# Part of one block's load moved to GpSimd's DMA queue, with unequal shares for the DMA engines

## The chip, the cores and the metric

The kernel runs on one core of one Trainium2 chip. Five engines work beside each other: TensorE (PE, matrix products), VectorE (DVE), ScalarE (ACT), GpSimd (POOL) and SyncE (SP). Data moves between HBM and the on-chip memory SBUF through 16 DMA engines, which all queues of the core share. The metric is the device time in microseconds (us); lower is better.

## The reference

A linear layer with a low-rank update whose weights are normalised by column and rescaled, applied to 32768 rows of 256 numbers:

```
W_adapted = W + scale * (lora_A @ lora_B)          # 256x256, rank 16
W_norm    = sqrt(sum(W_adapted**2, axis=0) + 1e-8)
W_final   = W_adapted / W_norm * m
y         = x.reshape(-1, 256) @ W_final           # x: 16 x 2048 x 256, float32
```

The weights are small. x is 32 MB and y is 32 MB, both in float32, and each is moved once.

## The kernel before, in words

The 32768 rows are cut into 8 blocks of 4096 rows (4 MB). In a block each of the 128 partitions holds 32 consecutive rows of 1 KB. A chunk is 4 of these rows on all partitions, so a block has 8 chunks, and the kernel counts 64 chunks in all; two chunks are a pair. SBUF has five block buffers (`x_bufs`). A result is written over the rows that it came from, so blocks 0 to 4 have fresh buffers, and block 5 can only be loaded when block 0 has been stored.

For each pair of chunks GpSimd rounds the rows to bfloat16 (L208), TensorE transposes them (L321), VectorE copies the transposed rows from PSUM (L248), TensorE multiplies them by the final weights (L335), and ScalarE copies the result over the rows of x (L276). The final weights are computed at the start.

The order of the transfers is written out by hand. All loads go on SyncE's queue (L169 to L178), in the order of the list `loads` (L111 to L114), whose entries are a first chunk, a number of chunks and the rows of one transfer. All stores go on ScalarE's queue (`stores`, L116 to L122, whose fourth entry is the chunk after which they are issued). With `H` = 40 (the first chunk of block 5), block 4 is loaded as six chunks in one transfer of 24 rows, then, after SyncE has waited for store 0 (block 0), as two transfers of 4 rows:

```
loads += [(H - CH, 6, 6 * J), (H - 2, 2, J)]
...
if loads[n][0] == H - 2:
    wait_store(nc.sync, 0)
```

The loads of blocks 5 to 7 follow on the same queue, behind that wait and further ones. GpSimd goes through the pairs in order (L193). Before a pair it waits for the load of its chunks where a new load begins (L196), and at pair `REST` = 15 it waits for store 2 (L204), which holds back the rest of the computation while transfers go on. At the end SyncE waits for the last stores (L359). Eight and 24 waits that hold nothing up lengthen the programs of GpSimd and VectorE (L255).

Of the kernel before, what the change touches and what calls it, by code (L numbers as in the profile page):

```python
# [11 lines left out]
def kernel(  # L12
# [10 lines left out]
    nc = tc.nc  # L23
    P = 128
# [5 lines left out]
    x_flat = x.flatten_outer_dims()  # L30
    out_flat = out.flatten_outer_dims()
    N, IN = x_flat.shape
# [3 lines left out]
    J = 4  # L36
    DJ = 32
# [5 lines left out]
    XBUFS = 5  # L43
    CH = DJ // J
# [4 lines left out]
    NXB = 2  # L49

    REST = 15
    NXT = 2
    F8 = 2 * J * P

# [7 lines left out]
    def sb(name, shape, dtype):  # L62
        return ctx.enter_context(nc.sbuf_tensor(name, shape, dtype))
# [4 lines left out]
    x_bufs = [sb(f"x_sb{k}", [P, DJ, IN], FP32) for k in range(XBUFS)]  # L68
    xb_bufs = [sb(f"xb{k}", [P, 2 * J, IN], BF16) for k in range(NXB)]
    xt_bufs = [sb(f"xt{k}", [P, F8, KC], BF16) for k in range(NXT)]  # L70
    w_nat = sb("w_nat", [P, KC, OUT], FP32)
# [38 lines left out]
    H = XBUFS * CH  # L110
    loads = [(0, 2, 2 * J), (2, 2, 2 * J), (4, 4, 4 * J)]  # L111
    loads += [(b * CH, CH, CH * J) for b in range(1, XBUFS - 1)]
    loads += [(H - CH, 6, 6 * J), (H - 2, 2, J)]
    loads += [(g0, 4, 4 * J) for g0 in range(H, NCH, 4)]  # L114
    load_of = {g: n for n, (g0, cnt, _) in enumerate(loads) for g in range(g0, g0 + cnt)}
    stores = [(b * CH, CH, CH * J, 19 + b) for b in range(F - 1)]  # L116
# [7 lines left out]
    def pieces(entry):  # L124

        return 16 * (entry[1] * J // entry[2])
# [5 lines left out]
    def sem(name):  # L132
        if name not in sems:
            sems[name] = tc.alloc_semaphore(name)
        return sems[name]

    def transfer(engine, name, entry, dram, store):
        g0, cnt, rows = entry[:3]
        b, c = divmod(g0, CH)
        (u0, ucnt), = [u for u in units if u[0] <= g0 < u[0] + u[1]]  # L140
        unit = dram[u0 * J * P : (u0 + ucnt) * J * P].rearrange("(p j) k -> p j k", p=P)
        for r in range(0, cnt * J, rows):
            here = x_bufs[b % XBUFS][:, c * J + r : c * J + r + rows, :]
            there = unit[:, (g0 - u0) * J + r : (g0 - u0) * J + r + rows, :]
            src, dst = (here, there) if store else (there, here)
            engine.dma_start(out=dst, in_=src).then_inc(sem(name), 16)

    def load_x(n):
        transfer(nc.sync, f"load{n}", loads[n], x_flat, False)

    def store_y(n):
        transfer(nc.scalar, f"store{n}", stores[n], out_flat, True)

    def wait_load(engine, g):
        engine.wait_ge(sem(f"load{load_of[g]}"), pieces(loads[load_of[g]]))

    def wait_store(engine, n):
        engine.wait_ge(sem(f"store{n}"), pieces(stores[n]))
# [3 lines left out]
        out=w_nat[:], in_=W.rearrange("(p t) o -> p t o", t=KC)  # L162
    ).then_inc(sem("load_w"), 16)
    nc.scalar.dma_start(
        out=a_nat[:], in_=lora_A.rearrange("(p t) r -> p t r", t=KC)
# [2 lines left out]
    nc.scalar.dma_start(out=m_row[:], in_=m[None, :]).then_inc(sem("load_m"), 16)  # L168
    for n in range(len(loads)):  # L169

        if loads[n][0] == H - 2:
            wait_store(nc.sync, 0)
        if loads[n][0] == H + CH:
            wait_store(nc.sync, 1)
        if loads[n][0] == H + 2 * CH:
            wait_store(nc.sync, 2)
            wait_store(nc.sync, 3)
        load_x(n)  # L178
# [5 lines left out]
        out=identity[:],  # L184
        in_=zeros[:],
# [7 lines left out]
    for p in range(1, NPR):  # L193
        b, c = divmod(p, PRB)
        for g in (2 * p, 2 * p + 1):
            if g == 2 or load_of[g - 1] != load_of[g]:  # L196
                wait_load(nc.gpsimd, g)


        if p == 1:  # L200
            nc.gpsimd.wait_ge(sem("dve"), 6)
        if p == 2:
            nc.gpsimd.wait_ge(sem("dve"), 8)
        if p == REST:  # L204
            wait_store(nc.gpsimd, FIRST - 2)
        if p >= NXB:
            nc.gpsimd.wait_ge(sem("turned"), p - NXB + 1)
        nc.gpsimd.tensor_copy(  # L208
            out=xb_bufs[p % NXB][:],
            in_=x_bufs[b % XBUFS][:, 2 * c * J : 2 * (c + 1) * J, :],  # L210
        ).then_inc(sem("rounded"), 1)
# [14 lines left out]
        out=wa[:], in0=ab_ps, scalar=float(scale), in1=w_nat[:], op0=ALU.mult, op1=ALU.add  # L226
# [19 lines left out]
    for p in range(NPR):  # L246
        nc.vector.wait_ge(sem("turned"), p + 1)
        nc.vector.tensor_copy(  # L248
            out=xt_bufs[p % NXT][:].rearrange("p r t -> p (r t)").bitcast(FP32),
            in_=xt_ps[p % 2][:],  # L250
# [4 lines left out]
    for engine, idle in ((nc.gpsimd, 8), (nc.vector, 24)):  # L255
# [13 lines left out]
        out=norm[:], in_=n2_ps, func=AF.Sqrt, bias=eps_col[:]  # L269
    ).then_inc(sem("act"), 1)  # L270
    drains = 0
    for g in range(NCH):
        b, c = divmod(g, CH)
        nc.scalar.wait_ge(sem("product"), g + 1)

        nc.scalar.copy(  # L276
            out=x_bufs[b % XBUFS][:, c * J : (c + 1) * J, :], in_=y_ps[g % 2][:]
        ).then_inc(sem("room"), 1)
        due = [n for n in range(len(stores)) if stores[n][3] == g]
        if due:  # L280
            drains += 1
            nc.scalar.drain().then_inc(sem("done"), 1)  # L282
            nc.scalar.wait_ge(sem("done"), drains)
            for n in due:
                store_y(n)
# [42 lines left out]
    def product(p):  # L328
        take("copied")
        for h in range(2):  # L330
            take("room")
            for t in range(KC):
                for j in j_order:
                    r = (h * J + j) * P
                    i = nc.tensor.matmul(  # L335
                        y_ps[h][:, j, :],
                        xt_bufs[p % NXT][:, r : r + P, t],
                        w_final[:, t, :],
# [57 lines left out]
```

## Time and profile before

| | before |
|---|---|
| median of 6 runs | 163.06 us (162.31 to 163.44) |
| profiled execution, time | 162.48 us |
| profiled execution, span | 161.2 us |
| TensorE, VectorE, ScalarE, GpSimd busy | 96.1, 45.0, 66.0, 60.9 us |
| moved by DMA | 67.43 MB, mean 418 GB/s |
| mean granted TensorE clock | 0.832 |

The span runs from the first to the last instruction of the program; the execution's time includes 1.28 us around it. A digit in a strip of the page is the busy share of one of 40 equal slices of the span, in tenths. The table of DMA queues gives packets, MB and the time that the packets took as a share of the 16 DMA engines' span: q1 carries SyncE's loads, q10 ScalarE's stores, and q14 the fetching of instructions. A line of waits names the engine, what it wanted to do next, and what ended the wait.

### The profile page before, as it was taken

The numbers are of one execution on the slowest core, as the hardware profiler recorded it, in microseconds if no ns is written. First come the engines' busy times: TensorE is split into PE (matmuls) and PEld (weight loads), VectorE is DVE, ScalarE is ACT, GpSimd is POOL, SyncE is SP. The second block draws the span as 40 slices with busy tenths as digits, with TensorE's granted clock in tenths as the row PEclk, the third lists the DMA queues.
The fourth block names the chain that finished last, engine by engine and source line by source line (L and its number), as shares of the span: only waits on it lengthen the run. The fifth ranks groups of instructions, "written<-read, shape, count | busy, mean of one in ns | idle before, by whom it ended". The sixth has DMA issues, their size and how long they took to land. (4 is left out here: it accounts for less than half of the span.)

```text
span 161.2 us, 2027 instructions
## 1 busy us (share of the span) xinstructions
PE 96.1 (60%) x786; PEld 84.5 (52%) x786; DVE 45.0 (28%) x44; ACT 66.0 (41%) x68; POOL 60.9 (38%) x38
## 2 busy tenths in 40 slices
PE   0795926999999720000799999989998910000000
PEld 0374915899998610000689999979977910000000
DVE  0666411435444500000214445345443300000000
ACT  3412640686777450000057686777775640000000
POOL 1045319668684000002938676755739000000000
PEclk9999996999999985555569999999999996555555
DMA  4999999999999999999999999999999999999995
GB/s 155 429 466 455 390 480 431 390 464 447 423 390 472 407 398 454 414 406 440 436 408 424 430 433 425 425 435 424 431 483 415 407 474 409 415 480 407 403 435 228
DMA packets 4645, 67.43 MB, mean 418 GB/s; under 512 B 657, under 2 KB 674, under 8 KB 1698
## 3 DMA queue, kind: packets, MB, share of 16 engines
q1 hardware_dynamic: 2304, 33.82, 49.2%
q10 hardware_dynamic: 2338, 33.59, 48.9%
q14 instruction: 3, 0.02, 0.0%
HBM read 33.85 MB, written 33.55 MB: 418 GB/s over the span
## 5 line engine op out<-in xcount | busy, mean ns | idle before, releaser
L276 ACT COPY x_sb<-y_ps 128x1024 f32<-128x1024 f32 x64 | 62.2, 1015 | 58.9 <-PE y_ps L335 57.1
L208 POOL CAST xb<-x_sb 128x2048 bf16<-128x2048 f32 x31 | 58.4, 1893 | 63.3 <-DMA x_sb<-in_x_dram 24.7
L335 PE MATMUL y_ps<-w_final,xt 128*128 128x256 bf16 x512 | 64.0, 279 | 3.7 <-PEq L311 3.6
L248 DVE COPY xt<-xt_ps 128x1024 f32<-128x1024 f32 x32 | 39.1, 1224 | 75.2 <-PE xt_ps L321 75.1
L335 PEld LDWEIGHTS y_ps<-w_final,xt 128*128 128x128 bf16 x512 | 51.1, 100 | 11.1 <-issue 4.6
L321 PE MATMUL xt_ps<-identity,xb 128*128 128x128 f32 x264 | 37.5, 289 | 25.2 <-PEq L311 25.1
L321 PEld LDWEIGHTS xt_ps<-identity,xb 128*128 128x128 f32 x264 | 32.5, 151 | 27.2 <-issue 26.7
L264 ACT CAST xb<-x_sb 128x2048 bf16<-128x2048 f32 x1 | 1.9, 1898 | 2.5 <-DMA x_sb<-in_x_dram 2.5
L292 PE MATMUL y_ps<-identity,a_nat 128*16 128x128 f32 x2 | 0.6, 394 | 3.6 <-DMA a_nat<-in_lora_A_dram 3.6
L262 ACT ACT_TABLE_LOAD x1 | 1.3, 1283 | 2.4 <-issue 2.4
L238 DVE RECIPROCAL rnorm<-norm 128x256 f32<-128x256 f32 x1 | 1.8, 1753 | 1.3 <-ACT norm L268 1.3
L305 PE MATMUL y_ps<-sq,ones 128*128 128x256 f32 x4 | 2.1, 674 | 0.0
L292 PEld LDWEIGHTS y_ps<-identity,a_nat 128*16 128x16 f32 x2 | 0.1, 90 | 3.6 <-issue 3.6
L214 POOL MEMSET xb<- 128x2048 bf16 x1 | 1.8, 1804 | 0.0
L305 PEld LDWEIGHTS y_ps<-sq,ones 128*128 128x128 f32 x4 | 1.2, 324 | 0.8 <-DVE sq L229 0.7
L301 PE MATMUL y_ps<-m_row,ones 1*128 1x256 f32 x2 | 1.2, 710 | 0.6 <-DMA m_row<-in_m_dram 0.6
L220 DVE CAST b_bf<-b_nat 16x256 bf16<-16x256 f32 x1 | 0.3, 281 | 2.9 <-DMA b_nat<-in_lora_B_dram 2.9
L301 PEld LDWEIGHTS y_ps<-m_row,ones 1*128 1x128 f32 x2 | 0.5, 306 | 1.1 <-DMA m_row<-in_m_dram 1.1
L296 PE MATMUL y_ps<-b_bf,aT 16*128 16x256 bf16 x2 | 0.6, 403 | 0.5 <-DVE aT L222 0.5
L225 DVE SCALAR_TENSOR_TENSOR wa<-y_ps,w_nat 128x512 f32<-128x512 f32 x1 | 0.7, 690 | 0.8 <-PE y_ps L296 0.8
L268 ACT ACTIVATE norm<-y_ps,eps_col 128x256 f32<-128x256 f32 x1 | 0.5, 475 | 0.9 <-PE y_ps L305 0.9
L241 DVE TENSOR_TENSOR w_final<-wam,rnorm 128x256 bf16<-128x256 f32 x2 | 0.8, 422 | 0.0
(14 smaller groups left out, 3.7 us busy)
## 6 DMA issues: line engine op xcount, KB each, us to landing
out_dram<-x_sb ACTq DMA_DIRECT2D x5, 4096.0 KB, 27.2
x_sb<-in_x_dram SPq DMA_DIRECT2D x7, 2048.0 KB, 29.5
x_sb<-in_x_dram SPq DMA_DIRECT2D x3, 4096.0 KB, 29.9
out_dram<-x_sb ACTq DMA_DIRECT2D x2, 2048.0 KB, 30.4
x_sb<-in_x_dram SPq DMA_DIRECT2D x1, 3072.0 KB, 46.1
out_dram<-x_sb ACTq DMA_DIRECT2D x2, 1536.0 KB, 19.4
out_dram<-x_sb ACTq DMA_DIRECT2D x1, 2560.0 KB, 30.8
out_dram<-x_sb ACTq DMA_DIRECT2D x5, 512.0 KB, 38.3
```

The source lines that it names most:

```text
L208: nc.gpsimd.tensor_copy(out=xb_bufs[p % NXB][:], in_=x_bufs[b % XBUFS][:, 2 * c * J : 2 * (c + 1) * J, :],).then_inc(sem("rounded"), 1)
L214: nc.gpsimd.memset(xb_bufs[NPR % NXB][:], 0.0).then_inc(sem("rounded"), 1)
L238: nc.vector.reciprocal(out=rnorm[:], in_=norm[:]).then_inc(dv, 1)
L241: i = nc.vector.tensor_mul(out=w_final[:, t], in0=wam[:, t], in1=rnorm[:])
L248: nc.vector.tensor_copy(out=xt_bufs[p % NXT][:].rearrange("p r t -> p (r t)").bitcast(FP32), in_=xt_ps[p % 2][:],).then_inc(sem("copied"), 1)
L262: nc.scalar.activation(out=warm[:], in_=eps_col[:], func=AF.Sqrt)
L264: nc.scalar.copy(out=xb_bufs[0][:], in_=x_bufs[0][:, 0 : 2 * J, :]).then_inc(sem("early"), 1)
L276: nc.scalar.copy(out=x_bufs[b % XBUFS][:, c * J : (c + 1) * J, :], in_=y_ps[g % 2][:]).then_inc(sem("room"), 1)
L301: nc.tensor.matmul(mb_ps, ones[0:1, :], m_row[:], start=True, stop=True).then_inc(pe, 1)
L305: i = nc.tensor.matmul(n2_ps, ones[:], sq[:, t, :], start=(t == 0), stop=(t == KC - 1))
L321: i = nc.tensor.transpose(xt_ps[p % 2][:, j * P : (j + 1) * P], xb_bufs[p % NXB][:, j, :].bitcast(FP32), identity[:],)
L335: i = nc.tensor.matmul(y_ps[h][:, j, :], xt_bufs[p % NXT][:, r : r + P, t], w_final[:, t, :], start=(t == 0 and (j % (J // 2)) == 0), stop ...
```

## The change

The last 12 rows of block 4 on each partition are loaded in another way. SyncE's first transfer of the block has 20 rows instead of 24. After the wait for store 0 it issues two transfers of 3 rows (rows 26 to 31). Rows 20 to 25 are loaded on GpSimd's own DMA queue, in three transfers that cover partitions 0 to 5, 6 to 125 and 126 to 127, issued ahead of GpSimd's wait at pair 15. GpSimd waits for both kinds before pair 18, whose second chunk begins at row 20. The amount of data is the same.

```
+    SIDE = 6
+    SHORT = 3
+    SHARES = ((0, 6), (6, 120), (126, 2))
...
-    loads += [(H - CH, 6, 6 * J), (H - 2, 2, J)]
+    loads += [(H - CH, 5, 5 * J)]
...
+    def load_end(engine, name, p0, cnt, r, rows, **kw):
+        unit = x_flat[(H - CH) * J * P : H * J * P].rearrange("(p j) k -> p j k", p=P)
+        engine.dma_start(
+            out=x_bufs[XBUFS - 1][p0 : p0 + cnt, r : r + rows, :],
+            in_=unit[p0 : p0 + cnt, r : r + rows, :],
+            **kw,
+        ).then_inc(sem(name), 16)
...
-        if loads[n][0] == H - 2:
+        if loads[n][0] == H:
             wait_store(nc.sync, 0)
+            for r in range(5 * J + SIDE, DJ, SHORT):
+                load_end(nc.sync, "short", 0, P, r, SHORT)
...
-            if g == 2 or load_of[g - 1] != load_of[g]:
+            if g in load_of and (g == 2 or load_of.get(g - 1) != load_of[g]):
                 wait_load(nc.gpsimd, g)
...
         if p == REST:
+            for k, (p0, cnt) in enumerate(SHARES):
+                load_end(
+                    nc.gpsimd, "side", p0, cnt, 5 * J, SIDE, max_dma_last_dim=SIDE * IN
+                )
             wait_store(nc.gpsimd, FIRST - 2)
+        if 2 * p < H - 3 <= 2 * p + 1:
+            nc.gpsimd.wait_ge(sem("side"), 16 * len(SHARES))
+            nc.gpsimd.wait_ge(sem("short"), 16 * ((3 * J - SIDE) // SHORT))
         if p >= NXB:
```

## The prediction

> **What bounds the kernel now.** I read the page's strip of DMA shares and its table of queues first, then the chain of waits, then the waits of GpSimd and of SyncE's queue, and last the windows and the packet and landing records at the very end. The page first:
>
> ```profile
> span 161.2 us, 2027 instructions
> ...
> DMA  4999999999999999999999999999999999999995
> GB/s 155 429 466 455 390 480 431 390 464 447 423 390 472 407 398 454 414 406 440 436 408 424 430 433 425 425 435 424 431 483 415 407 474 409 415 480 407 403 435 228
> DMA packets 4645, 67.43 MB, mean 418 GB/s; under 512 B 657, under 2 KB 674, under 8 KB 1698
> ...
> q1 hardware_dynamic: 2304, 33.82, 49.2%
> q10 hardware_dynamic: 2338, 33.59, 48.9%
> q14 instruction: 3, 0.02, 0.0%
> ```
>
> The 16 DMA engines are full from the second slice to the last but one, with loads (q1) and stores (q10) taking 98.1% of their time. The chain says the same from the other side: everything that is followed back by engine work is 5% of the span, and it ends at 130.9 us with the last store's issue.
>
> ```profile
> PE 4%; ACT 1%; ACTq 1%; issue 0%
> ```
>
> So compute has room: the last store is issued at 130.9 us and its first packets run at about 155, 24 us later. GpSimd sits in this wait in the middle (its cast of pair 14 ends at 51.03 us, the next starts at 75.52):
>
> ```profile
> POOL xb L208 <- DMA out_dram<-x_sb: 24.5, 1, 24.5
> ```
>
> The end is then set by the last DMA engine to finish its share. In windows as long as one 16 KB packet (columns: window and length, busy time of five engines, TensorE clock, DMA share, GB/s):
>
> ```profile
> 131.00:158.80 27.80, 0.00 (x0) 0.00 (x0) 0.00 (x0) 0.00 (x0) 0.00 (x0) 0.56 0.99 427
> 158.82:159.43 0.61, 0.00 (x0) 0.00 (x0) 0.00 (x0) 0.00 (x0) 0.00 (x0) 0.50 0.63 269
> 159.43:160.04 0.61, 0.00 (x0) 0.00 (x0) 0.00 (x0) 0.00 (x0) 0.00 (x0) 0.50 0.19 81
> 160.04:160.66 0.62, 0.00 (x0) 0.00 (x0) 0.00 (x0) 0.00 (x0) 0.00 (x0) 0.50 0.06 26
> 160.66:161.20 0.54, 0.00 (x0) 0.00 (x0) 0.00 (x0) 0.00 (x0) 0.00 (x0) 0.50 0.00 0
> ```
>
> One engine moves 427/16 = 27 GB/s. So 81 GB/s is three engines still at work, and 26 GB/s is one alone. The landing records of the last store agree: thirteen of its 16 increments come at 159.55 to 160.04 us, then 160.62, 160.68 and 161.13. Call the last A, the two before it B and C. Their packets, followed back by time, show why. B and C each let an 8 KB instruction fetch (q14) pass at 131.75 and 135.57 us and lose 0.66 and 0.40 us by it (309 ns, and a slower next packet: 1568 and 1306 instead of 1213 ns). A had no fetch then: while TensorE still worked, between 121.2 and 131.4 us, its eight 32 KB store packets took 1236 to 1312 instead of 1213 ns (+0.52 us in sum), with some 0.15 us more on the 12 KB packets before (474 to 491 instead of 460) and 0.18 on the two after. The trace numbers no engine, so which number A has, the profile doesn't tell.
>
> **What the Trainium skill says.** "DMA: Bandwidth & Descriptors", section "Why a DMA increments its semaphore by 16 and not by 1": a DMA runs on the largest number of engines up to 16 that divides its slowest dimension; on GpSimd's queue a number under 16 are consecutive engines from a cursor that goes round. The same place has an exception where 100 and 127 partitions ran on all 16 with the partitions rounded up per engine. No run here shows this yet. Its section "Queues, rings and completion order" says that each engine goes round its queues packet by packet; the trace agrees (at 100 us a 611 ns load packet and a 159 ns store packet alternate). "Latency and other measured facts" gives about 1 us to the first byte for GpSimd's path, and that page's fit has 2.0 us fixed for a DMA. "SBUF — State Buffer", section "SBUF: two separate sides", says that DMA slows where several DMA engines write one of the AXI ports; nothing before shows such a case.
>
> **The change, part by part.** Rows 20 to 31 of block 4 (12 KB per partition) came in two 4-row pieces and in the last 4 rows of the 24-row load. Now SyncE loads 20 rows, then two 3-row pieces (rows 26 to 31), and GpSimd loads rows 20 to 25 in three transfers of 6, 120 and 2 partitions. With the cursor at 0, 6 partitions go to engines 0 to 5, 120 go to fifteen engines from 6 round to 4, eight each, and the last 2 to engines 5 and 6. Bytes in all are unchanged; the share per engine is not:
> - The sixth engine (number 5) gets 2 instead of 8 partitions of these 6 rows: 6 x 6 KB = 36 KB less. A 16 KB packet comes every 607 ns, so 36/16 x 0.607 = 1.37 us less.
> - Engines 0 to 4 and 6 get a ninth partition: +6 KB, 0.23 us more. Engines 7 to 15 stay.
> - Packets: 24 data packets per engine for these rows become about 32 or 33 (20 KB x 8, 3 KB x 16, 6 KB x 8 or 9). From 155 ns per 4 KB and 607 ns per 16 KB, a packet costs 155 - 4/12 x 452 = 4.5 ns beside its bytes: 0.04 us, and two or three semaphore writes of 9 ns, 0.03 us. On all engines about 0.07 us.
>
> SyncE issues three loads before and three after, with the store wait between, so its queue is as long (328 to 1432 ns each, none on the path). Store 0, which landed at 60.05 us and releases them, has 32 KB per engine less ahead of it from the shorter load (1.19 us) and up to six 6 KB packets more beside it (1.4 us): +0.2 us. The loads of blocks 5 to 7 queue behind that wait; stores fill the engines meanwhile (99.6% on q10 from 50 to 62 us), so it costs nothing.
>
> GpSimd's three issues stand after the cast of pair 14, before the wait that lasts 24.5 us. The trace has no GpSimd DMA; between SyncE's 0.33 us and the skill's 2.0 us each they take 1 to 6 us, and I take 3. The wait covers all; without it each would push the casts of pairs 15 on, and TensorE with them, which still have the 24 us before the last stores. The side load's packets take turns with 1.21 us store packets: nine turns of 1.44 us, so it lands at about 67 us. Its new wait, and that on the short pieces (the old ones landed by 78.8), stands ahead of pair 18's cast, which began at 84.07 us; behind it on GpSimd are all later casts, and TensorE's turns wait for those. Some 5 us to spare; free.
>
> So the end moves with the last engine alone. If A is the sixth engine: 161.13 - 1.37 + 0.07 = 159.8, and B and C are last at 160.68 + 0.07, plus 0.23 where one of them has a ninth partition (6 of the other 15 do). In this execution the gain is 161.13 - 160.98 = 0.15 to 161.13 - 160.75 = 0.38 us, against its own time of 162.48 (span 161.2 and 1.28 around). The runs' median of 163.06 is 0.58 us higher. Every undisturbed packet here takes the same time to a few ns, so I look for those 0.58 us first in the engine that already is disturbed. If all of it is A's, the gain is 0.73 to 0.96 us; A then has 1.03 us to B, within the 1.37 taken off. I take 0.65, towards the upper half: **162.4 us**.
>
> **Rivals.** *A relieved, but B and C take over at once* (the profiled execution is typical, and the median's excess is common to all engines): gain 0.15 to 0.38, that is 162.7 to 162.9. For it: the 26 GB/s step is only 0.45 us long. Against: the profiled execution is at the fast end of 162.31 to 163.44.
>
> *The spared engine isn't the late one.* Either the cursor or the exception above spares another number, or A is late only through what the profiler writes. Then A keeps its time or gets 0.23 more: 163.1 to 163.4. For it: the trace has no engine numbers. Against: the cursor's rule fits 6, 120 and 2 exactly.
>
> *Slower: shared ports.* Eight consecutive partitions on an engine cross the grouping that the 128-partition loads keep, so two engines can write one SBUF port with side packets. At half speed nine packets of 0.23 us take 2.0 us more, and B or C end at about 162.8: +1.7 us, 164.7. Against: stores only read SBUF from 51 to 60 us, and the side load is a sixth of the traffic, so writes seldom meet. It decides from a loss on B or C of 0.49 us beyond the 0.15 to 0.38 that sparing A gives, about 0.75, some 85 ns on each of nine packets. A stall on fetching GpSimd's descriptors would have the same size and place.
>
> **How the numbers follow.** A measurement of this kernel tells about 0.3%, 0.49 us. Forecast 0.50 (161.9 to 162.57); B and C take over 0.20; wrong engine 0.10; slower 0.20. So faster 0.50, same 0.30, slower 0.20. The range: 161.8 leaves 0.05 below; above, 163.9 takes in both middle cases and the lesser port losses and leaves 0.12.
>
> **What would show it.** A GpSimd queue of 0.79 MB in the table; its issues near 51 us inside the 24 us wait; DMA share of 9 throughout; at the end the one-engine step of 26 GB/s gone or shorter, with two engines left last. Side packets well over 230 ns, or an engine still alone at the end, would make the prediction wrong, as would an instruction fetch newly placed on an engine that is late.

## The result, and the profile after

The changed kernel is slower: 164.12 us median (163.15 to 165.02) against 163.06 us, a ratio of 1.0072 with a 95% interval of 1.0056 to 1.0087. Its profiled execution took 164.33 us with a span of 163.0 us, 1.85 us more than that of before. It also spreads wider from run to run: 1.9 us from lowest to highest where the kernel before has 1.2.

The page of the changed kernel, the same parts as before:

```profile
span 163.0 us, 2030 instructions
...
DMA  4999998999999999989999999999999999999995
GB/s 167 422 448 450 442 458 386 466 434 394 442 450 386 386 411 449 405 314 454 400 434 419 436 428 422 437 428 421 419 469 435 404 452 434 410 466 410 414 422 217
DMA packets 4933, 67.43 MB, mean 414 GB/s; under 512 B 764, under 2 KB 789, under 8 KB 1986
...
q10 hardware_dynamic: 2338, 33.59, 49.1%
q1 hardware_dynamic: 2304, 33.03, 47.5%
q0 software_dynamic: 288, 0.79, 1.2%
q14 instruction: 3, 0.02, 0.0%
...
PE 4%; ACT 1%; ACTq 1%; issue 0%
```

The 0.79 MB are now on GpSimd's queue (q0). The bytes are the same, the DMA engines are as busy as before, and the chain still has under 6% of engine work, as before. The same bytes take longer. Where, the answer for GpSimd and the windows tell. GpSimd's three issues lie inside its wait, as foreseen, and cost it 2.0 us:

```profile
50.08 1.90 POOL L234 CAST xb<-x_sb 128x2048 bf16<-128x2048 f32 x1 [0.72 <-PE xt_ps L347]
51.92 2.02 POOL L160 DMA_DIRECT2D x_sb<-in_x_dram  x3
77.43 3.74 POOL L234 CAST xb<-x_sb 128x2048 bf16<-128x2048 f32 x2 [23.48 <-DMA out_dram<-x_sb]
```

The wait for store 2, though, ends at 77.4 instead of 75.5 us. Windows around the side load, before (first fence) and after (second); the last two columns are the DMA share and GB/s:

```profile
46.00:54.00 8.00, 7.89 (x74) 7.11 (x72) 3.68 (x3) 5.74 (x6) 3.79 (x2) 1.00 1.02 428
54.00:72.00 18.00, 2.49 (x22) 1.80 (x20) 1.23 (x1) 2.94 (x3) 0.00 (x0) 0.65 0.98 422
72.00:86.00 14.00, 8.44 (x52) 7.30 (x53) 2.45 (x2) 3.11 (x4) 7.52 (x4) 0.60 1.01 426
86.00:131.00 45.00, 42.02 (x382) 38.40 (x380) 18.36 (x15) 31.78 (x33) 26.25 (x14) 1.00 1.02 432
```

```profile
46.00:54.00 8.00, 7.89 (x73) 7.13 (x72) 3.55 (x4) 5.86 (x7) 6.57 (x6) 1.00 1.02 433
54.00:72.00 18.00, 3.43 (x30) 2.70 (x28) 1.39 (x2) 3.76 (x4) 0.00 (x0) 0.70 0.97 383
72.00:86.00 14.00, 6.53 (x35) 5.53 (x36) 1.25 (x2) 2.02 (x2) 5.63 (x3) 0.53 1.03 432
86.00:131.00 45.00, 43.63 (x399) 40.12 (x397) 19.57 (x16) 31.47 (x33) 28.18 (x15) 1.00 1.02 432
```

Only one row differs: from 54 to 72 us the engines move 383 instead of 422 GB/s at nearly the same share of busy time. That is 39 GB/s x 18 us = 0.70 MB, and at 418 GB/s it is 1.7 us, nearly all of the 1.85. Busy at a lower rate means longer packets. The packet records say which: the 256 store packets of 32 KB of stores 0 and 1, which run from 48.6 to 71.5 us, took 1303 ns on average instead of 1218, some up to 2111. Per engine, what they took over 1213 ns sums to 1.44 instead of 0.07 us. The side load's own packets were not slow: 158 packets of 4.5 KB took 178 to 185 ns.

The excess is not spread evenly. 0.32 of the 1.44 us had passed before the first side packet ran at 57.65 us, more than half of it in one turn at 54.8 us in which all 16 engines had packets of 1305 to 1526 ns. Another 0.63 us came in one turn at 69.3 us, again on all 16 engines at once (1681 to 2111 ns). Some of the loss is thus not made by a side packet running beside a store packet, and most of it strikes all engines together.

The end of the changed kernel, in windows of a packet's length:

```profile
160.40:161.04 0.64, 0.00 (x0) 0.00 (x0) 0.00 (x0) 0.00 (x0) 0.00 (x0) 0.50 0.48 205
161.04:161.65 0.61, 0.00 (x0) 0.00 (x0) 0.00 (x0) 0.00 (x0) 0.00 (x0) 0.50 0.19 81
161.65:162.25 0.60, 0.00 (x0) 0.00 (x0) 0.00 (x0) 0.00 (x0) 0.00 (x0) 0.50 0.07 27
162.25:163.00 0.75, 0.00 (x0) 0.00 (x0) 0.00 (x0) 0.00 (x0) 0.00 (x0) 0.50 0.00 0
```

The steps of 81 and 27 GB/s are there as before: one engine is still alone at the end. The landings of the last store run from 161.15 to 162.99 us, where they ran from 159.55 to 161.13. The first came 1.60 us later, the last 1.86. So two things went wrong: every engine lost about 1.6 us, and the last one was not relieved.

### The profile page after: what moved, and what is told of

It reads as the page before. It is cut to its first block, busy times and chain, and to the rows that moved or that the text cites. A ratio compares the mean times of both kernels' runs of the same rounds, so it can differ in the third digit from the quotient of the medians.

```text
span 163.0 us, 2030 instructions
## 1 busy us (share of the span) xinstructions
PE 97.2 (60%) x786; PEld 85.6 (53%) x786; DVE 45.0 (28%) x44; ACT 66.1 (41%) x68; POOL 62.9 (39%) x41
## 5 line engine op out<-in xcount | busy, mean ns | idle before, releaser
L361 PE MATMUL y_ps<-w_final,xt 128*128 128x256 bf16 x512 | 64.9, 282 | 3.5 <-PEq L337 3.4
L347 PEld LDWEIGHTS xt_ps<-identity,xb 128*128 128x128 f32 x264 | 33.1, 152 | 26.9 <-issue 26.3
L160 POOL DMA_DIRECT2D x_sb<-in_x_dram x3 | 2.0, 679 | 0.0
```

The lines of the kernel that those rows point to most:

```text
L160: engine.dma_start(out=x_bufs[XBUFS - 1][p0 : p0 + cnt, r : r + rows, :], in_=unit[p0 : p0 + cnt, r : r + rows, :], **kw,).then_inc(sem(na ...
L347: i = nc.tensor.transpose(xt_ps[p % 2][:, j * P : (j + 1) * P], xb_bufs[p % NXB][:, j, :].bitcast(FP32), identity[:],)
L361: i = nc.tensor.matmul(y_ps[h][:, j, :], xt_bufs[p % NXT][:, r : r + P, t], w_final[:, t, :], start=(t == 0 and (j % (J // 2)) == 0), stop ...
```

## The experiments

Two parts of the change can be taken apart: GpSimd's queue, and the split into shares by partitions.

**One transfer instead of the shares, on GpSimd's queue.**

```
-    SHARES = ((0, 6), (6, 120), (126, 2))
+    SHARES = ((0, 128),)
```

> The six rows still go on GpSimd's queue, but in one transfer of all 128 partitions, so each DMA engine should keep the partitions that it has in every other transfer and none is spared. Theory P (the loss comes from the 6, 120 and 2 split: partitions are written by another engine than the one that reads and writes them elsewhere): the slow store packets between 54 and 72 us go away, 163.1 us, within 0.3% of the kernel before. Theory Q (the loss comes from GpSimd's queue itself[...]): the store packets stay slow, 164.1 us or a little more, ratio about 1.007.

Measured 1.0042 (1.0022 to 1.0062), 163.57 us. Between the theories: over half of the loss stays without the split. Eight of its 22 runs, at 162.64 to 163.00 us, are as fast as the kernel before (162.90 us at the median beside it). In the window of the loss:

```profile
54.00:72.00 18.00, 3.13 (x28) 2.44 (x25) 1.23 (x1) 3.47 (x4) 0.00 (x0) 0.69 0.99 412
```

**The shares on SyncE's queue, and one transfer there.** SyncE issues the side load after the 14th transposed pair; GpSimd issues none. The control has `SHARES = ((0, 128),)` beside it.

```
         if loads[n][0] == H:
+            nc.sync.wait_ge(sem("turned"), 14)
+            for p0, cnt in SHARES:
+                load_end(nc.sync, "side", p0, cnt, 5 * J, SIDE, max_dma_last_dim=SIDE * IN)
             wait_store(nc.sync, 0)
```

> The same three shares of 6, 120 and 2 partitions, with the same descriptor length, on SyncE's queue instead of GpSimd's, issued at nearly the same moment (SyncE waits for the 14th transposed pair). Theory P: as slow as the changed kernel, 164 us or more, with store packets over 1213 ns beside the side load. Theory Q: 163.1 us, store packets at 1213 to 1220 ns.

> The six rows in one 128-partition transfer on SyncE's queue at the same moment: neither the split nor GpSimd's queue is left, only the cut of the block and the early issue. Theories P and Q both: 163.1 us, within 0.3% of before. If it is slow all the same, the cause is the cut into 20, 6, 3 and 3 rows or its place in time, and both theories fall.

The shares gave 1.0024 (1.0012 to 1.0036), the control 1.0005 (0.9995 to 1.0016). So the cut of the block and its place in time cost nothing that can be measured, and the shares cost something on SyncE's queue too. The control's window:

```profile
54.00:72.00 18.00, 2.97 (x26) 2.29 (x24) 1.22 (x1) 3.31 (x4) 0.00 (x0) 0.69 0.98 418
```

The store packets do not settle theory P here: in its profiled execution the control has them at 1249 ns on average, the shares at 1230. The control's excess lies almost all in the first turn of store 0, at 48 to 50 us (up to 2165 ns), before its side load runs. One thing spoilt the comparison: the limit on the last dimension acts in bytes. It cut the 6 KB of a partition into pieces of 1.5 KB, and on SyncE's queue every piece took a turn with a store packet, so that the side load was in flight until 81 us in the control and 83 us with the shares. The loads behind it were late and the time hardly moved, which shows how much room compute has. Another landing record is of use here: on SyncE's queue the shares leave one engine without any side packet, 48 KB or 1.8 us less, and in the last store one increment comes at 159.26 us with the middle of the others at 160.71. There sparing an engine seems to have put one ahead, by 1.45 us.

**The changed kernel with whole 6 KB pieces**, `max_dma_last_dim` left out.

> The changed kernel without its limit on the descriptor length, which cuts each partition's 6 KB into four pieces of 1.5 KB; now one piece per partition, a quarter of the descriptors on GpSimd's queue. Theory P: no change, 164.1 us. Theory Q: what is lost shrinks with the number of descriptors, 163.3 to 163.7 us.

Measured 1.0115 (1.0095 to 1.0135), from five runs. Theory Q as put there falls: a quarter of the descriptors did not make it better. Its profiled execution, at 163.36 us, lies 1.2 us and more under the other four and does not show the loss, so that the size is uncertain.

**Which engine is late?** In the kernel before, marks were added: small loads of 1 to 15 rows into a spare tile on SyncE's queue, each of its own size. In the trace their sets are nested: one engine carries all fifteen, the next those of 2 to 15 rows, and so on to one that carries none. Number k here is the engine that carries the marks of k + 1 rows and more. With fifteen marks after the last load:

```
+    def mark(k, slot):
+        n = 16 + 4 * (k if slot == k else k + 10)
+        nc.sync.dma_start(out=tags[0:k, slot, 0:n], in_=x_flat[0:k, 0:n]).then_inc(sem("mark"), 16)
...
+    for k in range(1, 16):
+        mark(k, k)
```

> The kernel before with marks, so that the trace tells the DMA engines' numbers: small loads of 1 to 15 rows into a spare tile, each of another size, the one of k rows on the k lowest engines; a 5-row and a 6-row one after store 0, all fifteen after the last load. The output is not touched. Theory L (the late engine is the sixth, number 5): the engine with the last landing carries the marks of 6 to 15 rows and none of 1 to 5. Theory W (the spared engine is another one): it carries a different set. Time near 163.2 us, the marks themselves cost the low engines up to 0.4 us.

> The changed kernel with the same marks. It tells three things: which number ended last, where number 5 ended, and what number 5's store packets took beside the side load. If sparing works as worked out, number 5 is about 1.4 us ahead of the others once the side load has landed (near 76 us). If it is eaten, number 5 is level with them, its store packets longer than theirs by about 1 us in sum. Time near 164.3 us.

> The six rows in one 128-partition transfer on GpSimd's queue, with the same marks. None is spared: number 5 is level with the others near 76 us and its store packets no longer than theirs; the engine that ends last is the same number as in the kernel before. Time near 163.7 us.

They took 163.66, 164.42 and 164.56 us, one run each. In the kernel before, the packets that end last, followed back by time, carry the marks of 5 to 15 rows: that is number 4, the fifth engine. Its store packets are the long ones of the prediction again (about 0.5 us over between 121 and 133 us). The packets with the marks of 6 to 15 rows, number 5, ended 1.75 us earlier and had nothing of it. With the whole transfer on GpSimd's queue the same signature was again on number 4, which ended second to last; number 0, with all the marks, was last. The two engines with late instruction fetches carried the sets of numbers 2 and 3. In the changed kernel the signature is on number 4 too, but it ended third from last, 0.4 us ahead of the last one: what ends last there is not what the prediction calls A. Two engines whose packets start within a few ns can change places in such a following, so these ends are less sure than the sets of marks.

In the changed kernel with marks, the five engines that have a first-share packet near 57 us carry both early marks (5 and 6 rows). The engine with the 6-row mark alone has no packet of the 120-partition share: number 5 was spared, as the rule of the cursor in the prediction says. Its store packets from 59.6 to 68.1 us took 1302, 1395, 1435, 1422, 1472 and 1435 ns, where most engines had 1214 to 1240 in these turns.

The changed kernel without marks shows the pattern turn by turn, on the one engine that has no side packet from 59.3 to 69.5 us. In five turns its store packets took 1411, 1539, 1412, 1424 and 1389 ns. The other engines took about 1246, 1347, 1240, 1227 and 1213 ns for theirs and 178 ns for a side packet, in sum 1424, 1525, 1418, 1405 and 1391. So the spared engine kept step with the others, and the relief was largely eaten: store 2's sixteen landings lie from 76.55 to 77.37 us, with none ahead by anything like 1.37.

The late reading was repeated with marks of 1 to 6 rows alone.

> The kernel before with marks of 1 to 6 rows after the last load, which tell engines 0 to 5 apart and cost them less than the full set: once more, which number ends last? Theory N: number 4 (marks of 5 and 6 rows, none of 1 to 4). If it is number 5 (the mark of 6 rows alone), the earlier reading falls.

It took 162.68 us. The signature (0.53 us over between 121 and 133 us) was on the packets with the marks of 5 and 6 rows, number 4 again. It ended second to last, 0.18 us ahead of one without any mark, which is a number of 6 or more. Number 4 has the long packets in every execution marked; it is the last one in one of the four.

**The whole transfer at the start**, ahead of GpSimd's first cast, where only loads run.

> One 128-partition transfer of the six rows on GpSimd's queue, issued at the very start (2 us), when only loads run, instead of at 52 us beside the stores. Theory S (GpSimd's queue costs time only beside the stores, whose packets it makes longer): 162.9 to 163.1 us, within 0.2% of before. Theory D (a GpSimd transfer costs the DMA engines the same wherever it stands): ratio about 1.004, as with the whole transfer at 52 us.

Measured 1.0031 (1.0014 to 1.0047). Nearer to theory D, and not told apart from the 1.0042 at 52 us. But the runs fall in two groups, twelve at 162.87 to 163.14 us as theory S has it and ten at 163.50 to 164.22, so that neither theory fits.

**Sparing the right engine.**

```
-    SHARES = ((0, 6), (6, 120), (126, 2))
+    SHARES = ((0, 5), (5, 120), (125, 3))
```

> Shares of 5, 120 and 3 partitions instead of 6, 120 and 2: by the rule of the cursor this spares engine number 4, which carried the marks of the late engine, instead of number 5. Theory N (the change spares the neighbour of the late engine, and sparing the right one works): the late engine falls back by some 1.4 us and the end is set by the next ones, 0.3 to 0.45% better than the changed kernel, ratio to before 1.003 to 1.004. Theory M (what sparing takes off an engine on GpSimd's queue is lost again on its longer store packets): as the changed kernel, 1.006 to 1.008.

Measured 1.0057 (1.0035 to 1.0078). Not told apart from the changed kernel: if sparing number 4 gains, it is about 0.15%, less than theory N wanted.

**Sparing the low engines**, with `SIDE = 3` and `SHARES = ((0, 5), (5, 121), (126, 2))`.

> Three rows instead of six on GpSimd's queue, in shares of 5, 121 and 2 partitions: engines 1 to 4 (the late one and those that carried the instruction fetches) take 1 or 2 partitions, engines 5 to 15 eleven or twelve. Theory N: the four late engines fall back by some 0.7 us, the others come up by 0.34; with half of the loss that the whole transfer on GpSimd's queue showed (0.2%) the ratio is 0.997 to 1.001. Theory M: 1.003 to 1.006.

Measured 1.0081 (1.0060 to 1.0103), with half of the bytes on GpSimd's queue. Theory N falls, and the loss lies at or above the top of theory M's range: it did not shrink with the bytes. The window shows the same drop as the changed kernel:

```profile
54.00:72.00 18.00, 3.46 (x31) 2.72 (x28) 1.41 (x2) 3.79 (x4) 0.07 (x1) 0.70 0.97 386
```

**A tiny load on GpSimd's queue** in the kernel before.

```
+        if p == REST + 5:
+            nc.gpsimd.wait_ge(sem("tiny"), 16)
         if p == REST:
+            nc.gpsimd.dma_start(out=tiny[:], in_=x_flat[0:P, 0:16]).then_inc(sem("tiny"), 16)
```

> The kernel before with one tiny load on GpSimd's queue at pair 15: 64 bytes on each of 128 partitions into a spare tile, 8 KB in all. Theory D1 (the loss comes with the use of GpSimd's queue, whatever it moves): ratio about 1.004, as with the whole transfer. Theory D2 (it comes with the bytes and descriptors moved there): 1.000, within 0.1%.

Measured 1.0003 (0.9988 to 1.0018): using the queue for so little costs nothing that can be measured.

**Split and queue taken apart once more.** The shares and two halves, `SHARES = ((0, 64), (64, 64))`, on SyncE's queue in pieces of 6 KB; the whole transfer on GpSimd's queue in pieces of 6 KB; the halves on GpSimd's queue in pieces of 1.5 KB.

> The shares of 6, 120 and 2 partitions on SyncE's queue, in pieces of 6 KB, so that the side load passes in about 10 us beside the stores as it does on GpSimd's queue (with 1.5 KB pieces it took turns with them until 82 us). Theory P (the split makes the store packets longer on any queue): ratio 1.004 or more, the 32 KB packets of stores 0 and 1 at 1250 ns or more on average. Theory X (it takes the split and GpSimd's queue together): 1.000 to 1.003, packets at 1215 to 1230 ns.

> The two halves of 64 partitions on SyncE's queue, in pieces of 6 KB: crossing without GpSimd's queue and without unequal bytes. Theory P: 1.004 or more, long store packets. Theory X: within 0.1% of before, store packets at 1215 to 1230 ns.

> One 128-partition transfer on GpSimd's queue in pieces of 6 KB, a quarter of the descriptors. If what the whole transfer costs there (0.42%) comes from its descriptors: 1.001 to 1.002. If from its bytes being on a third queue: 1.004.

> The six rows on GpSimd's queue in two transfers of 64 partitions: every engine again gets 8 partitions in all and none is spared, but half of them are other engines' partitions. Theory X (crossing partitions on GpSimd's queue): as the changed kernel or worse, ratio 1.006 to 1.010, with the 32 KB store packets at 1280 ns or more. If crossing is not it but the unequal shares are: as the whole transfer, 1.003 to 1.005.

Measured 1.0049 (1.0029 to 1.0069), 1.0032 (1.0009 to 1.0055), 1.0025 (1.0001 to 1.0049) and 1.0074 (1.0046 to 1.0102), in this order. The first says again that the shares cost on SyncE's queue. The 32 KB store packets of its profiled execution average 1255 ns over both stores, little more than the control's 1249; counted from 54 us on they average 1264, the control's 1222. The window has

```profile
54.00:72.00 18.00, 3.27 (x29) 2.56 (x26) 1.23 (x2) 3.60 (x4) 0.00 (x0) 0.69 0.98 406
```

In this execution too one engine has no side packet, and it kept step again: 1428 to 1485 ns for its store packets from 58.7 to 66 us, where the others took 1213 to 1261 ns and 234 ns for a 6 KB side packet. None is ahead in the last store, whose first landings are at 160.84, 160.86 and 160.87 us, though this one had 1.8 us less to do.

The second lies between the theories. The fourth, with eight partitions for every engine and none spared, is as slow as the changed kernel. So it is probably neither the sparing nor unequal bytes that costs most; its interval, from six runs, still meets that of the whole transfer (1.0022 to 1.0062). Its profiled execution took 162.80 us, well under its median of 163.99, and does not show the loss (packets of 1222 ns, against the 1280 expected); the verdict rests on the times. The third, whose median is that of the kernel before, leaves open how much a whole transfer on GpSimd's queue costs: five of its 22 runs are at 164.6 us and more. That one, in its profiled execution, had the window of a kernel without loss:

```profile
54.00:72.00 18.00, 1.03 (x8) 0.71 (x8) 0.39 (x1) 2.94 (x3) 0.00 (x0) 0.62 0.98 419
```

**Three transfers without a split**, two rows each on all 128 partitions, on SyncE's queue:

```
-            for p0, cnt in SHARES:
-                load_end(nc.sync, "side", p0, cnt, 5 * J, SIDE)
+            for r in range(5 * J, 5 * J + SIDE, 2):
+                load_end(nc.sync, "side", 0, P, r, 2)
```

> The six rows on SyncE's queue in three transfers as with the shares, but each of 2 rows on all 128 partitions: three transfers, no split by partitions. If the split by partitions is what costs (Theory P): 0.999 to 1.0015. If the mere number of transfers is (three instead of one): 1.003 to 1.005, as the shares on SyncE's queue.

Measured 1.0014 (1.0003 to 1.0026), below the whole interval of the shares in pieces of 6 KB, but not told apart from the shares in pieces of 1.5 KB (1.0012 to 1.0036), and its own pieces are of 2 KB. So what the number of transfers costs and what the split by partitions costs is not fully separated. Its store packets average 1260 ns, again with the excess in the first turn of store 0 (up to 2351 ns), before the side load.

The ratios together, each to the kernel before in runs beside it:

| side load | SyncE's queue | GpSimd's queue |
|---|---|---|
| one transfer of 128 partitions, 1.5 KB pieces | 1.0005 | 1.0042 |
| one transfer of 128 partitions, 6 KB pieces | not run | 1.0025 |
| three transfers of 128 partitions, 2 KB pieces | 1.0014 | not run |
| two halves of 64 partitions | 1.0032 (6 KB) | 1.0074 (1.5 KB) |
| shares of 6, 120 and 2 | 1.0024 (1.5 KB), 1.0049 (6 KB) | 1.0072 (1.5 KB), 1.0115 (6 KB, five runs) |

Split and queue each cost, and together they make the loss: with pieces of 1.5 KB, both the shares on SyncE's queue (1.0024) and the whole transfer on GpSimd's (1.0042) lie above the control (1.0005); the three ran in the same batch, with medians of 163.22, 163.57 and 162.94 us. Why the store packets get longer is not shown. One guess is that an engine which takes other partitions than in the 128-partition transfers disturbs an engine that is reading a store from the same part of SBUF. The spared engine's long packets may fit that. The turns in which all 16 engines are slow at once do not, least of all the one before the first side packet, nor do the slow first turns of stores without a split. What the GpSimd queue adds for a whole transfer, and why only in some runs, stays open. No version beat the kernel before.

## Why the prediction was wrong

- **What bounds the kernel** held. The sum of what the 16 engines do sets the end, and compute has room: even with GpSimd's last casts 11 us later (130.85 instead of 119.61 us, in the control on SyncE's queue) the time moved by 0.05%.
- **The side load's mechanics** held: the cursor spared number 5; GpSimd's issues (3 us taken, 2.0 measured) lay inside the wait; the new waits cost nothing. That the side load lands at 67 us was off: its packets held three pieces of 1.5 KB instead of a whole 6 KB, ran only from 57.65 us, and the last landed at 76.7.
- **"If A is the sixth engine"** failed. The engine with A's long packets carries the marks of number 4, and by the cursor's rule number 4 even got the ninth partition, 0.23 us more. Sparing number 4 instead brought 1.0057, so the right number would not have saved the forecast. The text said that the trace numbers no engine, and the forecast still gave the spared number being the late one most of the chance. That was the rival "the spared engine isn't the late one", held at 0.10.
- **The term "on all engines about 0.07 us"** failed by far more: the landings of the last store show 1.60 us on the first engine and 1.59 us in the middle. It counted the packets that the change adds (its 4.5 ns for a packet beside the bytes come out at 4.3, which changes nothing) and took the packets of the stores as fixed, since they were fixed in the trace of before. They are not: 1303 instead of 1218 ns, 1.37 us per engine. This is the step that made the kernel slower.
- **The slower rival** was in the right place, from 54 to 72 us, and of about the right size (2.0 us priced for nine packets, 164.7 us, against 1.37 us of longer store packets and 164.12 us). But its mechanism, side packets slowed where two engines write a port, did not happen: they keep their length, and the store packets are the long ones, in part before any side packet runs. That its size came near is luck. The stall on GpSimd's descriptors, named with it, no run tests. The point from which it decides, 0.75 us, was passed.
- **Relief of 1.37 us** for the spared engine failed as well. While the side load ran, the spared engine's store packet took as long as the others' store and side packet together (1389 to 1539 ns against 1391 to 1525), and none was ahead at store 2's landings. What is taken off one engine is not gained where it keeps step with the rest; why it does is open.
- **The 0.58 us between the profiled execution and the median** were given to A without a trace for it. In the marked kernel before, 1.18 us slower than that execution, the first landing of the last store came 0.52 us later, at 160.07 us: there, excess of this size was common to all engines, as the rival with B and C had it.

## What to carry to other kernels

Where all DMA engines are full, packet times read off a trace hold for the pattern of that trace: here 1213 ns, the same to a few ns before, became 1303 on average once the pattern changed, so a change of pattern needs a price for the packets that it does not touch. Bytes taken off one engine were not time taken off it here while it kept step with the others (1412 ns for its store packet alone, 1240 and 178 for theirs). Before an engine is relieved by number, find out its number, by small marked loads whose sets of engines are nested. And when the last engine is only 0.45 us behind the next two, a cost common to all 16 of half a microsecond ends any gain.

## What was not expected of the hardware

- Side packets of 4.5 KB kept 178 to 185 ns, while 32 KB store packets on the same engines went from 1213 to as much as 2111 ns, on all 16 engines in the same turn.
- The engine without side packets kept step with the others, with side packets of 178 ns (changed kernel) and of 234 ns (shares on SyncE's queue in 6 KB pieces).
- The first packets of store 0 took up to 2165 and 2351 ns in two executions without split or GpSimd queue, before any side packet.
- The same 0.79 MB on GpSimd's queue cost 0.25 to 0.42% as one transfer of 128 partitions, but 8 KB there cost nothing (1.0003), and these transfers spread the runs from 162.45 to 164.93 us.
- Longer pieces (6 KB instead of 1.5 KB) did not make the split shares faster: 1.0115 (five runs) instead of 1.0072 on GpSimd's queue, and 1.0049 instead of 1.0024 on SyncE's, where the intervals overlap.
- The engine with the long packets between 121 and 133 us is the fifth in each of the four marked executions. They do not go with TensorE's work alone: in the kernel before its last product ends at 129.7 us, and this engine's packets are long until 134.
